# Banded attention's output: one bank-wide copy, two stored halves, and a later sum in memory

## The chip, the cores and the metric

The kernel runs on one core of a Trainium2 chip. The core has five engines that run beside each other and wait for one another by semaphores: TensorE (PE, with its weight loads shown apart as PEld), VectorE (DVE), ScalarE (ACT), GpSimd (POOL) and SyncE (SP). In this kernel SP alone issues the memory transfers (DMAs), strictly in order, and sixteen DMA engines carry them out. PSUM is the small memory that TensorE writes and that DVE and ACT read; SBUF is the working memory of 128 partitions; DRAM is the large memory outside. The metric is device time in microseconds (us).

## The reference

The kernel computes one decoder layer on 2048 tokens of width 1024 behind 16 meta tokens. Cut to what matters:

```python
xn = rms_norm(h, norm_gain[l])
proj = xn @ w_in[l]
sb_q, sb_k, sb_v, sw_q, sw_k, sw_v, sb_z, sw_z, g_sb, g_sw = jnp.split(proj, offsets, axis=-1)
o_sb = stick_breaking_attention(sb_q, sb_k, sb_v, valid)              # 8 heads of 64
o_sw = sliding_window_sink_attention(q, k, sw_v, attn_sinks[l], valid) # 16 query heads, 2 kv heads
y_sb = (o_sb * jax.nn.silu(sb_z)) @ w_branch_sb[l]
y_sw = (o_sw * jax.nn.silu(sw_z)) @ w_branch_swa[l]
merged = jax.nn.sigmoid(g_sb) * y_sb + jax.nn.sigmoid(g_sw) * y_sw
h = h + merged @ w_out[l]
return rms_norm(h, final_norm_gain)[:, BLOCK:]
```

The change concerns `o_sw`, the banded attention's output before it is gated by `sw_z`: within a block of 128 queries, probabilities over the block and the one before it, times the values, for 16 heads of 64.

## The kernel before, in words

All matrix products run on TensorE in three passes: every operand is split into a rounded high part and a low part (the remainder), and high times high, high times low and low times high are added up in one PSUM bank of 128 partitions by 512 columns. The tokens are four groups `g` of 512, taken in two halves: half 0 is groups 2 and 3, half 1 is groups 0 and 1 (the sequence is stored backwards, so half 0 is the end with the meta tokens).

The stages, in the order of the program: a start (projections for the first keys, values and queries); the banded attention of half 0 (`window`, woven among projections); the stick-breaking attention of half 0 (`stick`, woven among the gate projections); the remaining gates of half 0; the banded attention of half 1; the stick-breaking attention of half 1; the last gates of half 1; and `finish`, which takes half 0 (groups 2 and 3) and then half 1 through the branch projections, the output projection and the last norm.

What sets the order of the work: TensorE's order is fixed by the program text (`weave` mixes a main and a side stream by estimated costs), in the whole kernel. The orders of DVE, ACT, POOL and SP are chosen when the kernel is built, by a planner that follows a simulated timeline, except at the start, where they are partly written out. On the chip each engine then takes its instructions strictly in that order, so an instruction that waits holds all behind it. Tiles of one name rotate through a fixed number of buffers (`bufs`); a new tile waits until the buffer's last reader is done.

The banded attention works in units (head set `s` of four heads, group `g`, block `i`), 64 in all, 32 in each half. A unit goes through `scores` (products in bank `z`, copies to `sc` on ACT and DVE, maximum and exponentials, L691 to L716), three units later through `turn` (transposes in bank `t`, the split into `ph` and `pl`, L736 to L747) and then `values` (L749 to L773): six matmuls (L761) fill the single PSUM bank `o`. The value operand holds high parts in 64 columns and low parts in the other 64, so that bank rows 0 to 63 are the product with the high values and rows 64 to 127 that with the low values; their sum is the output. ACT copies rows 64 to 127 to SBUF (L763), and two DVE additions (L767), one for each parity of the head, add rows 0 to 63 and write the tile `os` (128 by 2 by 512, one buffer). After the fourth unit of a group two DMAs of 256 KB store `os` to the DRAM tiles `ow`, of which there are 32 (head pair `k` of 8, group `g` of 4). The next unit's matmuls need the bank `o` back, that is, both additions done.

`gated` (L194) later loads an `ow` tile and its gate `zw`, multiplies them and splits the product into the projection's operands. It does this for half 0's sixteen tiles during the last gates of half 1, and for half 1's sixteen in `finish`, after each half-0 group's output. For the stick-breaking output `od`, which is stored as a high and a low tile (L201 adds them), it does the same with one load and one DVE addition more.

`finish` runs, for half 0: 16 branch projections of 24 matmuls (d of 8, g of 2), multiplied by the gate `gt` loaded from `gw` (L259), with all of `gated(od)` at d = 3; then 16 projections of 12 matmuls, multiplied and merged (L267, L268, L270, L271), each d followed by a load and a split of an output weight tile (`out_weights`, L242 and L243); then the output products (L288 to L290). Staging tiles `a` have six buffers (AB), `gt` three; PSUM results rotate over six banks.

In `stick`, `row` makes a row of scores (L862, L866) and scans it on DVE (L876), five rows ahead of `turn` in half 1, and `tmp` tiles (nine buffers) serve as staging.

Of the kernel before, what the change touches and what calls it, by code (L numbers as in the profile page):

```python
# [7 lines left out]
F32 = mybir.dt.float32  # L8
# [3 lines left out]
ALU = mybir.AluOpType  # L12
# [4 lines left out]
P = 128  # L17
# [4 lines left out]
GT = 512  # L22
# [11 lines left out]
AB = 6  # L34
# [13 lines left out]
def tile_kernel(ctx, tc, x, xt, meta, metat, gain, w_in, w_sb, w_sw, w_out, sinks, fgain,  # L48
# [6 lines left out]
    V, A, G, T = nc.vector, nc.scalar, nc.gpsimd, nc.tensor  # L55

    def DMA(dst, src):
        nc.sync.dma_start(*(t.bitcast(F32) if t.dtype == F32R else t for t in (dst, src)))
# [28 lines left out]
    def dram(name, shape, dt=F32):  # L87
        return dp.tile(shape, dt, tag=name, name=name)
# [6 lines left out]
    gs = [[dram(f"gs{p}_{g}", [P, GT]) for g in range(4)] for p in range(8)]  # L95
    gw = [[dram(f"gw{p}_{g}", [P, GT]) for g in range(4)] for p in range(8)]
    od = [[dram(f"od{p}_{g}", [2, P, GT]) for g in range(4)] for p in range(4)]
    ow = [[dram(f"ow{p}_{g}", [P, GT]) for g in range(4)] for p in range(8)]
    ksv = dram("ksv", [P, 4, P], F32R)
    msd = [dram(f"msd{p}", [NM, P]) for p in range(2)]  # L100
    vsv = dram("vsv", [P, 2 * P], F32R)
# [88 lines left out]
    def rings():  # L190
        lp = cst.enter_context(tc.tile_pool(name="cl", bufs=1, side="left"))
        return lambda dt=F32R: lp.tile([P, GT], dt, tag="L", name="ringl", bufs=32)

    def gated(src, zz, k, g, ring, stg):  # L194

        a, b = stg(), stg()
        if src is od:
            c = stg()
            DMA(a, src[k][g][0])
            DMA(c, src[k][g][1])  # L200
            V.tensor_tensor(a, a, c, op=ALU.add)  # L201
        else:
            DMA(a, src[k][g])
        DMA(b, zz[k][g])
        V.tensor_tensor(a, a, b, op=ALU.mult)
        h, l = ring(), ring()
        A.copy(h, a)
        V.tensor_tensor(l, a, f32(h), op=ALU.subtract)
        return h, l

    def finish(ringl, osw, first):
# [6 lines left out]
        def ringr(dt=F32R):  # L218
            return cp.tile([P, GT], dt, tag="R", name="ringr", bufs=32)
# [7 lines left out]
        def project(acc, ws, ox):  # L227
            nk = len(ox)
            for k in range(nk):
# [2 lines left out]
                T.matmul(acc, lhsT=wh[:, k, :], rhs=l, start=False, stop=False)  # L232
                T.matmul(acc, lhsT=wl[:, k, :], rhs=h, start=False, stop=k == nk - 1)  # L233

        for half, groups in enumerate(halves):
            part, merged, wo = {}, {}, {}

# [10 lines left out]
            for d, g in order:  # L248
                if d == 3 and g == groups[0]:
                    osb = {(k, g): gated(od, zs, k, g, ringr, lambda: small("a", AB)) for g in groups for k in range(4)}  # L250
                if d not in ws_of:
                    ws_of[d] = first if half == d == 0 else weights(d * P, w_sw)
                ws = ws_of[d]
                acc = bank()
                project(acc, ws, [osw[k, g] for k in range(8)])
                gt = small("gt", 3)
                DMA(gt, gw[d][g])
                part[d, g] = ringr(F32)
                V.tensor_tensor(part[d, g], acc, gt, op=ALU.mult)  # L259
            for d in range(8):  # L260
                ws = weights(d * P, w_sb)
                for g in groups:
                    acc = bank()
                    project(acc, ws, [osb[k, g] for k in range(4)])
                    gt = small("gt", 3)
                    DMA(gt, gs[d][g])
                    V.tensor_tensor(gt, acc, gt, op=ALU.mult)  # L267
                    V.tensor_tensor(gt, gt, part[d, g], op=ALU.add)  # L268
                    mh, ml = merged[d, g] = ringl(), ringl()
                    A.copy(mh, gt)  # L270
                    V.tensor_tensor(ml, gt, f32(mh), op=ALU.subtract)  # L271
                out_weights(d, 0)
            for g in groups:
                for t0 in range(0, 4, 2):
# [33 lines left out]
                    for t in (t0, t0 + 1):  # L308
                        row = g * GT + t * P
                        if end and t == 3:  # L310
# [7 lines left out]
                            a, b = scaled_by[0], scaled_by[1]  # L318
# [23 lines left out]
    def tmp(dt=F32, rows=P):  # L342
        return tp.tile([rows, GT], dt, tag="tmp", name="tmp", bufs=9)
# [259 lines left out]
    def window(half, groups, sp):  # L603
# [145 lines left out]
        def values(s, g, i, st):  # L749
            kv = s // 2  # L750
            blk = 4 * (g - groups[0]) + i
            if i == 0:
                os_[0] = sp.tile([P, 2, GT], F32, tag="os", name="os", bufs=1)
            o = ps("o")
            ph, pl, pm = st["p"]
            oc = o.rearrange("p (a q) -> p a q", a=4)
            for n in range(2):
                c = slice(HB * n, HB * n + HB)
                v = vv[:, blk + n, kv, :]
                for j, (lv, rp) in enumerate(((v, ph), (v, pl), (dv[kv, blk][:, n, :], pm))):  # L760
                    T.matmul(oc[:, :, c], lhsT=lv, rhs=rp[:, :, c], start=j == 0, stop=j == 2)  # L761
            t = tmp(rows=64)
            A.copy(t, o[64:128])  # L763
            ov = o[0:64].rearrange("p (b a q) -> p b a q", b=2, a=2)
            tv = t.rearrange("p (b a q) -> p b a q", b=2, a=2)
            for a in range(2):
                V.tensor_tensor(os_[0][64 * a:64 * a + 64, :, i * P:(i + 1) * P],  # L767
                                ov[:, :, a, :], tv[:, :, a, :], op=ALU.add)
            if i == 3:
                for pr in range(2):  # L770
                    DMA(ow[2 * s + pr][g], os_[0][:, pr, :])

        os_ = [None]  # L773
        ending = []
# [21 lines left out]
        return sw_k, sw_v, sw_q, attend, ending  # L796


    def stick(groups, bp):
        kt, vc = {}, {}  # L800
        rows_of = {}
        lt = LT[groups[0] == 0]
# [30 lines left out]
        def load_q(h, g):  # L833
            p, a = divmod(h, 2)
            r = slice(64 * a, 64 * a + 64)
            q1 = bp.tile([P, GT], F32R, tag="q1", name="q1", bufs=2)
            q2 = bp.tile([P, GT], F32R, tag="q2", name="q2", bufs=2)
            for t in range(2):
                DMA(q1[64 * t:64 * t + 64], qd[p][g][t][r])
                DMA(q2[64 * t:64 * t + 64], qd[p][g][1 - t][r])  # L840
            return q1, q2

        state = {}

        def row(h, g, n, j):

            if n == j == 0:
                load_kv(h, g)
                state[h, g] = {"q": load_q(h, g), "last": {}}
            st = state[h, g]  # L850
            last = st["last"]
            b0 = 4 * (g + n) + j
            nb = min(4, NB - b0)
            end = b0 + nb == NB
            w = nb * P + (NM if end and nb < 4 else 0)
            k0 = (b0 - 4 * groups[0]) * P
            own = end and nb == 4
            z = ps("z")
            zm = ps("zm") if own else None
            for t, qt in enumerate(st["q"]):  # L860
                lq = qt[:, j * P:(j + 1) * P]
                T.matmul(z[:, :w], lhsT=lq, rhs=kt[h][:, k0:k0 + w], start=t == 0, stop=t == 1)  # L862
                if own:
                    T.matmul(zm[:, :NM], lhsT=lq, rhs=kt[h][:, k0 + w:k0 + w + NM], start=t == 0, stop=t == 1)
            r = bp.tile([P, RW], F32, tag="row", name="row", bufs=12)
            A.activation(r[:, :w], z[:, :w], AF.Sigmoid, scale=-1.0)  # L866
            if own:
                A.activation(r[:, w:w + NM], zm[:, :NM], AF.Sigmoid, scale=-1.0)
                w += NM
            if n == 0 and mask is None:  # L870
                G.affine_select(out=r[:, :P], in_=r[:, :P], pattern=[[1, P]], compare_op=ALU.is_ge,  # L871
                                fill=1.0, base=-1, channel_multiplier=-1)
            if n == 0 and mask is not None:
                V.tensor_tensor_scan(r[:, :w], r[:, :w], mask[:, :w], 1.0, op0=ALU.mult, op1=ALU.max)  # L874
            else:
                V.tensor_tensor_scan(r[:, :w], r[:, :w], r[:, :w], last[j] if n else 1.0, op0=ALU.mult, op1=ALU.min)  # L876
            last[j] = r[:, w - 1:w]
            rows_of[h, g, n, j] = r
# [44 lines left out]
        n = len(steps)  # L923
        turned = []
        for s in range(n + lt + 3):
# [3 lines left out]
            t = s - lt  # L929
# [164 lines left out]
    halves = ([2, 3], [0, 1])  # L1094
# [160 lines left out]
    for half, groups in enumerate(halves):  # L1255
        gts = [lambda spec=spec: gate(*spec) for spec in specs[half]]
        with tc.tile_pool(name=f"swa{half}", bufs=1, side="left") as sp:
# [13 lines left out]
            q = [[lambda p=p: sw_q(p) for p in (2 * s, 2 * s + 1)] for s in range(4)]  # L1271
# [22 lines left out]
            else:  # L1294
                for mk, gs_ in ((sw_k, groups), (sw_v, groups), *((f, groups[:1]) for f in q[0])):
                    w, use, _ = mk()
# [6 lines left out]
            side = attend()  # L1303
# [8 lines left out]
            early = first_sums(*groups, short)  # L1312
        with tc.tile_pool(name=f"sb{half}", bufs=1, side="left") as bp:
            hsplit[0], vsplit[0] = True, False
            side = stick(groups, bp)
            drain(tiles_by_tile(gts[few:few + 1], groups))
            rest = 28 - FAST - PLAIN if half == 0 else 23
            cost_sb = 8 * sum(4 * (4 - g) for g in groups) * 1.31 + 16 * 0.75 + LT[half] * 0.86
            ratio = cost_sb / ((rest - few - 1) * 10.4)
            weave(tiles_by_tile(gts[few + 1:rest], groups), side, ratio)  # L1320
            if half == 0:
                hsplit[0] = vsplit[0] = True
                plain = [mk() for mk in gts[rest:rest + 2]]
            drain(side)
        if half == 0:
            with tc.tile_pool(name="fast", bufs=1, side="left") as bp:
                pairs = list(zip(specs[0][-FAST::2], specs[0][-FAST + 1::2]))
                sums_x = combined(*groups, bp, short, *early)
                with tc.manual_schedule(engines={mybir.EngineType.Activation}):
                    for n in range(PLAIN):  # L1330
                        w, use, _ = plain[n]
# [86 lines left out]
```

## Time and profile before

| what | value |
|---|---|
| median of three runs | 2139.83 us (2138.06 to 2143.08) |
| the profiled execution | 2139.65 us |
| its span (first to last instruction) | 2138.0 us |
| PE busy | 2111.4 us (99%) |
| DVE busy | 1460.2 us (68%) |
| ACT busy | 1078.6 us (50%) |
| POOL busy | 307.7 us (14%) |
| DMA traffic | 390.93 MB, mean 183 GB/s |
| granted TensorE clock | full in all stages |

The profile page gives busy times, a row for each group of instructions and the chain of work that ended last. The trace behind it answers for any stretch of the span (in us from its start), any line or any tile. A wait is named by what ended it. Matmuls overlap: one of 512 columns reads 0.39 us, while the next may start 0.23 us after it. Half 0's banded attention lies at about 100 to 373 us, half 1's at 840 to 1104, half 1's stick-breaking at 1104 to 1615, half 0's part of `finish` at 1683 to 1880.

### The profile page before, as it was taken

What the parts mean: (1) busy time and instruction counts of PE and PEld (TensorE: products, weight loads), DVE (VectorE), ACT (ScalarE), POOL (GpSimd) and SP (SyncE); (2) the same over time, 40 slices, a digit from 0 to 9 for tenths busy, and PEclk for the clock granted to TensorE, in tenths of its full rate; (3) what the DMA queues carried; (4) which work ended last, traced back from release to release, by engine and by line L of the source; (5) the groups of instructions that cost most, each with busy time, mean ns of one, the idle gap of its engine ahead of it and who ended that gap; (6) DMA issues with size and microseconds to landing.
All of it is one profiled execution on the core that took longest, in us unless ns stands there. A gap on an engine that the chain in (4) does not pass through costs nothing.

```text
span 2138.0 us, 30784 instructions
## 1 busy us (share of the span) xinstructions
PE 2111.4 (99%) x10658; PEld 1751.4 (82%) x10658; DVE 1460.2 (68%) x2335; ACT 1078.6 (50%) x2461; POOL 307.7 (14%) x494
## 2 busy tenths in 40 slices
PE   8999999999999999999999999999999999999998
PEld 6788888888888888888888888888888888787886
DVE  7788876878887554777738888877774447454553
ACT  6576775555546335777735555555553213221121
POOL 2234453111000001343310000000000121000000
PEclk9999999999999999999999999999999999999999
DMA  9755554756448574435354434333324986568422
GB/s 337 276 191 191 177 193 165 242 181 200 153 156 326 213 254 154 148 138 175 134 178 152 123 124 131 113 116 108 113 90 172 359 288 209 172 221 308 149 94 89
DMA packets 170043, 390.93 MB, mean 183 GB/s; under 512 B 24448, under 2 KB 28288, under 8 KB 169888
## 3 DMA queue, kind: packets, MB, share of 16 engines
q1 hardware_dynamic: 169888, 388.97, 54.0%
q8 instruction: 84, 1.38, 0.3%
q14 instruction: 71, 0.58, 0.1%
HBM read 241.55 MB, written 145.18 MB: 181 GB/s over the span
## 4 chain that ended last, share of the span: by engine, by line
PE 84%; DVE 5%; ACT 4%; issue 3%; DMA 2%; POOL 1%; SPq 0%; POOLq 0%; ACTq 0%; DVEq 0%
PE ps_g L412 11%; PE ps_g L413 11%; PE ps_g L414 11%; PE ps_o L913 6%; PE ps_z L862 6%; PE ps_t L887 6%; PE ps_z L705 2%; PE ps_o L761 2%; PE ps_g L233 1%; PE ps_g L232 1%; PE ps_g L231 1%; PE ps_z L233 1%; PE ps_z L231 1%; PE ps_z L232 1%; PE ps_t L233 1%
## 5 line engine op out<-in xcount | busy, mean ns | idle before, releaser
L412 PE MATMUL ps_g<-xh,wh 128*128 128x512 f32 x1296 | 532.9, 411 | 8.7 <-ACT xh L1107 6.8
L414 PE MATMUL ps_g<-xh,wl 128*128 128x512 f32 x1296 | 509.7, 393 | 0.6 <-DVE wl L111 0.6
L413 PE MATMUL ps_g<-xl,wh 128*128 128x512 f32 x1296 | 509.2, 393 | 0.0
L876 DVE TENSOR_TENSOR_SCAN row<-row 128x512 f32<-128x512 f32 (+4 forms) x256 | 293.6, 1147 | 93.3 <-ACT row L866 40.3
L414 PEld LDWEIGHTS ps_g<-xh,wl 128*128 128x128 f32 x1296 | 243.8, 188 | 55.6 <-DVE wl L111 1.1
L412 PEld LDWEIGHTS ps_g<-xh,wh 128*128 128x128 f32 x1296 | 244.9, 189 | 48.5 <-ACT xh L1107 6.8
L866 ACT ACTIVATE row<-ps_z 128x512 f32<-128x512 f32 (+1 forms) x320 | 172.4, 539 | 211.8 <-PE ps_z L862 191.4
L413 PEld LDWEIGHTS ps_g<-xl,wh 128*128 128x128 f32 x1296 | 245.1, 189 | 38.2 <-DVE xl L1108 1.3
L114 ACT ACTIVATE wth<-ps_t 128x512 fp32r<-128x512 f32 (+1 forms) x320 | 170.6, 533 | 75.8 <-PE ps_t L887 74.0
L115 DVE SCALAR_TENSOR_TENSOR wtl<-ps_t,wth 128x512 fp32r<-128x512 f32 (+1 forms) x320 | 189.1, 591 | 25.5 <-ACT wth L114 25.1
L862 PE MATMUL ps_z<-kt,q 128*128 128x512 f32 (+3 forms) x640 | 185.5, 370 | 0.0
L887 PE MATMUL ps_t<-ident,row 128*128 128x128 f32 x1088 | 171.6, 273 | 0.1
L887 PEld LDWEIGHTS ps_t<-ident,row 128*128 128x128 f32 x1088 | 134.6, 140 | 33.7 <-DVE wtl L115 0.8
L862 PEld LDWEIGHTS ps_z<-kt,q 128*128 128x128 f32 x640 | 117.9, 188 | 23.8
L913 PE MATMUL ps_o<-wth,vc 128*128 128x512 f32 (+1 forms) x320 | 130.3, 407 | 0.2
L913 PE MATMUL ps_o<-wtl,vc 128*128 128x512 f32 (+1 forms) x320 | 116.7, 365 | 0.0
L713 ACT ACTIVATE sc<-sc,nm 128x129 f32<-128x129 f32 x256 | 100.0, 393 | 31.4 <-DVE nm L711 30.3
L111 POOL TENSOR_TENSOR wl<-raw,wh 128x1024 fp32r<-128x1024 f32 (+1 forms) x28 | 60.3, 2155 | 325.4 <-ACT wh L108 287.6
L871 POOL TENSOR_SCALAR_AFFINE_SELECT row<-row 128x128 f32<-128x128 f32 x64 | 20.3, 318 | 469.4 <-ACT row L866 442.2
L108 ACT CAST wh<-raw 128x1024 fp32r<-128x1024 f32 (+1 forms) x44 | 42.7, 971 | 87.9 <-PE ps_g L232 35.5
L874 DVE TENSOR_TENSOR_SCAN row<-row,mask 128x512 f32<-128x512 f32 (+2 forms) x64 | 67.9, 1066 | 19.6 <-ACT row L866 11.5
L567 ACT ACTIVATE tmp<-ps_g 128x512 f32<-128x512 f32 x84 | 50.2, 598 | 61.6 <-PE ps_g L414 55.3
(435 smaller groups left out, 4118.0 us busy)
## 6 DMA issues: line engine op xcount, KB each, us to landing
wh<-h_in_w_in SPq DMA_DIRECT2D x66, 512.0 KB, 3.6
wl<-l_in_w_in SPq DMA_DIRECT2D x66, 512.0 KB, 4.8
raw<-in_w_in SPq DMA_DIRECT2D x50, 512.0 KB, 5.6
h_in_w_in<-wh SPq DMA_DIRECT2D x50, 512.0 KB, 2.9
l_in_w_in<-wl SPq DMA_DIRECT2D x50, 512.0 KB, 4.0
q<-qd SPq DMA_DIRECT2D x128, 128.0 KB, 3.1
vc<-vd SPq DMA_DIRECT2D x48, 256.0 KB, 2.9
kd<-tmp SPq DMA_DIRECT2D x32, 256.0 KB, 3.8
```

What stands on the lines that cost most here:

```text
L114: A.activation(h, acc, AF.Copy, scale=scale)
L115: V.scalar_tensor_tensor(l, acc, scale, f32(h), op0=ALU.mult, op1=ALU.subtract)
L412: T.matmul(acc, lhsT=wh[:, k, :], rhs=xh[g][:, k, :], start=k == 0, stop=False)
L413: T.matmul(acc, lhsT=wh[:, k, :], rhs=xl[g][:, k, :], start=False, stop=False)
L414: T.matmul(acc, lhsT=wl[:, k, :], rhs=xh[g][:, k, :], start=False, stop=k == KT - 1)
L713: A.activation(sc[:, hh, :], sc[:, hh, :], AF.Exp, bias=nm[:, hh:hh + 1], accum_out=den[:, hh:hh + 1])
L862: T.matmul(z[:, :w], lhsT=lq, rhs=kt[h][:, k0:k0 + w], start=t == 0, stop=t == 1)
L866: A.activation(r[:, :w], z[:, :w], AF.Sigmoid, scale=-1.0)
L874: V.tensor_tensor_scan(r[:, :w], r[:, :w], mask[:, :w], 1.0, op0=ALU.mult, op1=ALU.max)
L876: V.tensor_tensor_scan(r[:, :w], r[:, :w], r[:, :w], last[j] if n else 1.0, op0=ALU.mult, op1=ALU.min)
L887: T.transpose(tr[:, j * P:(j + 1) * P], rows_of[h, g, n - (j > i), j][:, k0:k0 + P], ident)
L913: T.matmul(o[:, :n], lhsT=v, rhs=r, start=first and r is wh, stop=last)
```

## The change

In `values`, ACT copies the whole bank (128 by 512) at once into `os`, which now has the shape 128 by 4 heads by 256 columns (two units, the same number of bytes, still one buffer). The 64-row copy and both DVE additions are gone. After every second unit four DMAs of 128 KB each (64 partitions, runs of 1 KB) store the high rows to `ow[k][g][0]` and the low rows to `ow[k][g][1]`; the `ow` tiles are twice as large.

A new function `closed` loads both parts of one `ow` tile (256 KB each), adds them on DVE and stores the sum over the high part (256 KB). It is called 32 times. Half 0's sixteen tiles are closed in half 1's `stick`, in `row`, at the starts of head and group pairs: none at the first two, two at the third, one at each later one and one more at the eighth. Half 1's sixteen are closed in half 0's part of `finish`: eight in the branch loop for d of 4 to 7 (one for each d and group), eight in the merge loop, one for each d. `gated` then loads part 0 as it did before.

```diff
-    ow = [[dram(f"ow{p}_{g}", [P, GT]) for g in range(4)] for p in range(8)]
+    ow = [[dram(f"ow{p}_{g}", [2, P, GT]) for g in range(4)] for p in range(8)]
...
+    def closed(k, g, stg):
+
+        a, b = stg(), stg()
+        DMA(a, ow[k][g][0])
+        DMA(b, ow[k][g][1])
+        V.tensor_tensor(a, a, b, op=ALU.add)
+        DMA(ow[k][g][0], a)
+
     def gated(src, zz, k, g, ring, stg):
 
         a, b = stg(), stg()
+        DMA(a, src[k][g][0])
         if src is od:
             c = stg()
-            DMA(a, src[k][g][0])
             DMA(c, src[k][g][1])
             V.tensor_tensor(a, a, c, op=ALU.add)
-        else:
-            DMA(a, src[k][g])
...
+        open_ = [(k, g) for g in halves[1] for k in range(8)]
...
                 DMA(gt, gw[d][g])
+                if half == 0 and d > 3:
+                    closed(*open_.pop(0), lambda: small("a", AB))
...
                     V.tensor_tensor(gt, gt, part[d, g], op=ALU.add)
+                    if half == 0 and g == groups[0]:
+                        closed(*open_.pop(0), lambda: small("a", AB))
...
-            if i == 0:
-                os_[0] = sp.tile([P, 2, GT], F32, tag="os", name="os", bufs=1)
+            if i % 2 == 0:
+                os_[0] = sp.tile([P, 4, 2 * P], F32, tag="os", name="os", bufs=1)
...
-            t = tmp(rows=64)
-            A.copy(t, o[64:128])
-            ov = o[0:64].rearrange("p (b a q) -> p b a q", b=2, a=2)
-            tv = t.rearrange("p (b a q) -> p b a q", b=2, a=2)
-            for a in range(2):
-                V.tensor_tensor(os_[0][64 * a:64 * a + 64, :, i * P:(i + 1) * P],
-                                ov[:, :, a, :], tv[:, :, a, :], op=ALU.add)
-            if i == 3:
+            A.copy(os_[0][:, :, i % 2 * P:(i % 2 + 1) * P], oc)
+            if i % 2:
                 for pr in range(2):
-                    DMA(ow[2 * s + pr][g], os_[0][:, pr, :])
+                    for n in range(2):
+                        DMA(ow[2 * s + pr][g][n][:, (i - 1) * P:(i + 1) * P].rearrange("(a d) t -> d a t", a=2),
+                            os_[0][64 * n:64 * n + 64, 2 * pr:2 * pr + 2, :])
...
-    def stick(groups, bp):
+    def stick(groups, bp, open_=()):
+        open_ = list(open_)
...
                 state[h, g] = {"q": load_q(h, g), "last": {}}
+                for t in open_[:(0, 0, 2, 1)[min(len(state) - 1, 3)] + (len(state) == 8)]:
+                    closed(*t, tmp)
+                    open_.remove(t)
...
-            side = stick(groups, bp)
+            side = stick(groups, bp, half * [(k, g) for g in halves[0] for k in range(8)])
```

## The prediction

> **What bounds the kernel now.** I read the page first (busy times, then the chain that ended last), then busy times by stage, then what TensorE (PE) waited for in the two banded stages, then the chain around single waits. From the page, the busy line and the chain's shares:
>
> ```profile
> PE 2111.4 (99%) x10658; PEld 1751.4 (82%) x10658; DVE 1460.2 (68%) x2335; ACT 1078.6 (50%) x2461; POOL 307.7 (14%) x494
> ...
> PE 84%; DVE 5%; ACT 4%; issue 3%; DMA 2%; POOL 1%; SPq 0%; POOLq 0%; ACTq 0%; DVEq 0%
> ```
>
> TensorE is the bound: 99% busy, 84% of the chain. Its work and order do not change, so a gain can only come out of its waits. Where these lie, the busy times by stage show (us, then busy time and count of PE, PEld, DVE, ACT and POOL, the granted clock, DMA share, GB/s): the banded attention of half 0 from its first output, that of half 1, half 1's stick-breaking, and in the finish the branch loop for d of 4 to 7 and the merge loop.
>
> ```profile
> 130.00:373.00 243.00, 238.96 (x1355) 204.34 (x1354) 190.11 (x375) 170.72 (x498) 108.58 (x185) 1.00 0.52 181
> 889.00:1104.00 215.00, 212.80 (x1172) 183.31 (x1171) 155.78 (x314) 152.81 (x434) 76.52 (x151) 1.00 0.43 147
> 1135.00:1615.00 480.00, 479.94 (x2607) 400.96 (x2606) 385.27 (x466) 264.02 (x515) 17.67 (x60) 1.00 0.37 113
> 1727.00:1772.00 45.00, 45.00 (x194) 36.22 (x193) 16.24 (x20) 5.78 (x9) 7.40 (x4) 1.00 0.66 231
> 1772.00:1817.00 45.00, 45.00 (x194) 36.09 (x193) 37.73 (x53) 16.01 (x28) 8.78 (x6) 1.00 0.72 234
> ```
>
> In the banded stages PE idles 4.04 and 2.20 us, 6.2 together; in the three others it does not idle by more than 0.06. What ended its idle times there, half 0 first, then half 1 (us in total, times, longest):
>
> ```profile
> PE ps_zm L525 <- DVE tmp L115: 1.8, 2, 1.1
> PE ps_o L761 <- DVE os L767: 0.8, 2, 0.6
> PE ps_t L551 <- DVE tmp L518: 0.7, 1, 0.7
> ```
>
> ```profile
> PE ps_o L761 <- DVE os L767: 1.6, 1, 1.6
> PE ps_o L761 <- POOL pm L745: 0.4, 2, 0.2
> ```
>
> The three waits on L767 are PE waiting for the bank `o`, which the two additions free. The chain around one of these shows an addition directly in front (start, us, what):
>
> ```profile
> 186.08 0.43 DVE os L767
> 186.51 0.14 issue
> 186.64 0.36 PE ps_o L761
> ```
>
> Busy rows hide a little of a stall: a matmul reads 0.39 us where the next can start 0.23 later, as two in a row in the finish do, so each wait is 0.16 longer than its idle time.
>
> ```profile
> 1811.68 0.39 PE L233 MATMUL ps_g<-ringr,wl 128*128 128x512 f32 x1
> 1811.91 0.39 PE L231 MATMUL ps_g<-ringr,wh 128*128 128x512 f32 x1
> ```
>
> **The change part by part.** The groups of the removed work, of the nearest copy of a whole bank, and of two additions like the new one (mean ns behind the comma):
>
> ```profile
> L767 DVE TENSOR_TENSOR os<-ps_o,tmp 64x256 f32<-64x256 f32 x128 | 52.8, 413 | 6.8 <-ACT tmp L763 5.8
> L763 ACT COPY tmp<-ps_o 64x512 f32<-64x512 f32 x64 | 37.4, 584 | 17.2 <-PE ps_o L761 15.9
> L917 ACT COPY tmp<-ps_o 128x512 f32<-128x512 f32 x32 | 18.8, 587 | 19.4 <-PE ps_o L913 19.1
> L205 DVE TENSOR_TENSOR a<-a 128x512 f32<-128x512 f32 x32 | 22.0, 689 | 9.2 <-DMA a<-zs 6.9 <-DMA a<-zw 2.0
> L201 DVE TENSOR_TENSOR a<-a 128x512 f32<-128x512 f32 x16 | 14.6, 914 | 12.4 <-DMA a<-od 12.4
> ```
>
> *Removed:* 128 additions by 413 ns, 52.8 us of DVE, all in the banded stages (about 345.9 us of DVE busy there). The bank comes back after the ACT copy alone, some 0.83 us earlier. The least that this is worth is the three waits on L767: 0.8 + 1.6 + 3 × 0.16 = 2.9 us. The most is all idle time of the two stages with 0.16 for each of the eight waits listed: 6.2 + 1.3 = 7.5 us. Other waits there end with DVE as well (the 1.8 on L115, 0.7 on L518), a smaller part with POOL; I take the middle, 5.2 us.
>
> *The wider copy:* 64 copies go from 584 to 587 ns, 0.2 us of ACT, beside PE's projections.
>
> *The stores:* 128 DMAs of 128 KB from 64 partitions instead of 32 of 256 KB. The nearest rows are `od`'s stores of the same size: their issue on SP (ns min/median/max), their landing (last figure, us), and for comparison the landing of the old stores (us min/median/max); then the shortest time between two copies that will have a store between them:
>
> ```profile
> L58 SPq DMA_DIRECT2D od<-tmp x64: 445/512/1115, 406.1 to 1628.2; - x64
> ```
>
> ```profile
> od<-tmp SPq DMA_DIRECT2D x64, 128.0 KB, 2.5
> ```
>
> ```profile
> DMA to landing us min/median/max: 2.0/2.2/3.6
> ```
>
> ```profile
> 313.96 0.59 ACT L763 COPY tmp<-ps_o 64x512 f32<-64x512 f32 x1
> ...
> 318.60 0.59 ACT L763 COPY tmp<-ps_o 64x512 f32<-64x512 f32 x1 [0.33 <-PE ps_o L761]
> ```
>
> `os` has one buffer, so the third unit's copy waits on ACT until the four stores of the pair before have landed: 0.59 for the copy, three issues of 0.51, 2.5 to land, 4.6 us from copy to copy. The shortest gap is 4.64 us; the mean is 243/32 = 7.6 us. So this costs 0, if SP takes the stores up at once. If they land in 3.6 us the need is 5.7, and 31 times the 1.1 us missing at the shortest gap would be 34 us of ACT: the far end, since few gaps are that short. What is queued behind the waiting copy on ACT is the next unit's `ph` and `sc` work, for which PE's transposes and matmuls wait. On SP 96 issues more by 0.51 us are 49 us, spread over 458 us. SP waited 3.4 us for each group before, so it stood ready:
>
> ```profile
> SPq L58 <- DVE os L767: 54.2, 16, 8.4
> ```
>
> *Half 0's sums in stick-breaking:* 16 additions by 0.69 us, 11.0 us on DVE, with 48 DMAs. DVE goes from 385 to 396 of 480 us. The tightest place is the start of a head and group pair, where the transposes follow the scan of the fourth row; one such place:
>
> ```profile
> 1340.39 1.23 DVE L876 TENSOR_TENSOR_SCAN row<-row 128x512 f32<-128x512 f32 x1 [0.96 <-POOL row L871]
> ```
>
> ```profile
> 1344.38 0.60 PE L887 MATMUL ps_t<-ident,row 128*128 128x128 f32 x4
> ```
>
> The scan ends at 1341.62, PE takes its row at about 1344.7: 3 us in hand, against one addition of 0.69. Cost 0; if nothing hid them, 11.0.
>
> *Half 1's sums in the finish:* eight additions in the branch loop, 5.5 us, where DVE idles 45 - 16.24 = 28.8 us: 0. Eight more in the merge loop, 5.5 us, where DVE idles only 7.3 us. And there its lateness is passed on, as the chain behind the loop shows:
>
> ```profile
> 1819.91 0.70 DVE ringl L271
> ...
> 1821.95 5.45 DMA a<-in_w_out
> ```
>
> ```profile
> 1830.02 0.50 PE L289 MATMUL ps_z<-ringr,ringl 128*128 128x512 f32 x1 [0.22 <-DVE ringr L243]
> ```
>
> SP issues the second half of the output weights only behind L271, and PE already waits for them at 1830. So DVE's lag at 1819.91 is paid one for one. Idle time ahead takes seven additions; the last has almost none behind it, so I charge one, 0.7 us (ends: 0 and 5.5). In this loop the sums move 8 × 0.786 MB, 140 GB/s more on 234; the heaviest stretch of the finish carried 385, so this fits, with nothing to spare:
>
> ```profile
> 1690.00:1700.00 10.00, 10.00 (x45) 8.04 (x44) 3.95 (x6) 0.00 (x0) 0.00 (x0) 1.00 1.04 385
> ```
>
> *Sum:* -5.2 for the banded stages, 0 for the copies, 0 for the stores, 0 in stick-breaking, +0.7 in the finish: -4.5 us, on the profiled execution's own 2139.65 (which stands 0.18 below the median): 2135.1 us. What is late next in the banded stages is POOL's `pm` (L745) and ACT's exponentials.
>
> A row that speaks against the change is L201: the same addition, 0.69 us alone, has a mean of 914 ns, and one of it reads
>
> ```profile
> 1716.73 2.89 DVE L201 TENSOR_TENSOR a<-a 128x512 f32<-128x512 f32 x1
> ```
>
> [...]
>
> **The rivals.**
>
> *All of these waits go* (chance 0.14): the earlier bank also lets ACT and POOL start earlier, as the additions stood ahead of so many waits, and the finish hides its sums: -7.5, 2132.1. Against it: the waits on POOL and ACT that are left.
>
> *The freed time does not reach PE* (0.14): only the three bank waits go, since the chain around the others passes to ACT (153 to 171 us busy per stage) and POOL: -2.9 + 0.7, 2137.4, within 0.2% (4.3 us, about what a measurement of this kernel can tell from no change).
>
> *The merge loop falls behind* (0.15): its additions meet POOL's weight splits. At 2.89 us each, eight are 23.1 us against 7.3 idle: a lag of 15.8, paid in full at 1830: -5.2 + 15.8 = +10.6, 2150. It decides for slower when the lag passes 9.5 us, that is from 2.1 us an addition. For it: L201's rows; against: POOL is busy in 8.78 of 45 us.
>
> *The stores hold ACT* (0.11): SP reaches them late, being held by another wait (its longest for `os` alone was 8.4). At 4 us late the need is 8.6 from copy to copy, 1.0 over the mean of 7.6: 31 us of ACT; a third of that on PE, 10 us, with the bank waits back: 2139.65 + 10 = about 2150. It decides from about 3 us late on.
>
> **How the numbers follow.** The forecast's own case (a gain of 3 to 7 us, 2132.7 to 2136.7) has 0.46; three quarters of it lie beyond 0.2%. Faster: 0.34 + 0.14 = 0.48. Within 0.2%: 0.12 + 0.14 = 0.26. Slower: 0.15 + 0.11 = 0.26. The range runs from below the case of all waits, 2130, to 2147, which takes in the milder part of both slower cases.
>
> **What would show it.** In the new profile L767 is gone, and 64 copies of 128x512 near 587 ns stand in its place; DVE's busy time in the banded stages falls by about 25 us each, PE's idle time there from 6.2 to 1 or 2, without a wait on `os` at L761. ACT waits for the `os` stores nowhere. In stick-breaking PE stays without idle time. In the finish the new additions read 0.7 to 0.9 us, L271's last stands within 1 us of where it stood relative to PE, and PE's wait near 1830 grows by less than 1 us. Wrong would be: ACT waiting for stores of `os`; PE waiting at L289 for L243 by several us; a DVE addition blocked on its loads ahead of scans; or new waits because the planner orders ACT, DVE and SP otherwise around the shorter DVE queue, which no row of before can price.

## The result, and the profile after

The changed kernel takes 2147.06 us (median of nine runs, 2144.11 to 2150.31) against 2139.83 for the kernel before on the same chip (nine runs, 2138.06 to 2143.82): a ratio of 1.0031, 95% interval 1.0022 to 1.0041. It became slower by 0.3%; 2135.1 was predicted, in a range from 2130 to 2147. The profiled execution took 2146.06 us, 6.41 more than that of before. The same statements stand up to 11 lines further down in the changed kernel (the bank's matmuls L761 at L772, the output products L288 to L290 at L299 to L301, the merges L267 to L271 at L276 to L282); L773 is the new copy, L199 the addition in `closed`.

First the busy times by stage of the changed kernel, for the five stretches that the prediction showed and two short ones behind them (columns: stretch, its length, busy time and count of PE, PEld, DVE, ACT and POOL, granted clock, DMA share, GB/s):

```profile
130.00:373.00 243.00, 240.41 (x1370) 206.64 (x1369) 171.93 (x317) 168.06 (x500) 110.41 (x186) 1.00 0.63 201
889.00:1104.00 215.00, 214.03 (x1178) 184.76 (x1177) 131.66 (x251) 147.97 (x432) 71.77 (x149) 1.00 0.54 171
1135.00:1615.00 480.00, 479.02 (x2603) 400.13 (x2602) 390.44 (x480) 263.59 (x512) 17.77 (x60) 1.00 0.44 138
1727.00:1772.00 45.00, 45.00 (x194) 36.22 (x193) 21.27 (x28) 4.67 (x7) 6.57 (x5) 1.00 0.90 326
1772.00:1817.00 45.00, 45.00 (x194) 36.08 (x193) 35.38 (x52) 14.58 (x24) 8.17 (x5) 1.00 1.00 357
1817.00:1825.00 8.00, 1.91 (x6) 0.70 (x5) 5.25 (x9) 2.10 (x4) 0.00 (x0) 0.87 0.85 319
1825.00:1832.00 7.00, 6.67 (x19) 4.81 (x20) 4.25 (x7) 2.15 (x5) 0.00 (x0) 0.66 0.68 209
```

In the two banded stages PE now idles 2.59 and 0.97 us, 3.56 instead of 6.2, and DVE is busy 18 and 24 us less. In stick-breaking PE idles 0.98 us instead of 0.06. The merge loop (1772 to 1817) moves 357 GB/s where it moved 234, and its DMA share is 1.00: the sixteen engines are busy all the time. Behind it PE is busy for 1.91 of 8 us.

What ended PE's idle times, in the order of the program: the two banded stages (shown there: only the waits of the `o` bank's matmuls, L772), stick-breaking, finish (us in total, times, longest):

```profile
PE ps_o L772 <- POOL pm L756: 0.8, 1, 0.8
...
PE ps_o L772 <- DVE pl L115: 0.7, 1, 0.7
PE ps_o L772 <- POOL pm L756: 0.2, 1, 0.2
...
PE ps_t L898 <- DVE wtl L115: 1.0, 1, 1.0
...
PE ps_t L299 <- ACT ringl L281: 6.3, 1, 6.3
```

The waits for the bank copy are gone, and one new wait of 6.3 us stands at the first output product that needs the last merged operand. PE executes the same 10658 matmuls in the same order in both kernels, so the start of one and the same matmul can be compared. In the two banded stages PE gains 3.25 and 1.67 us, 4.9 together; about 1.0 is lost again between the two, in a part that the change does not touch. At the end of half 1's banded attention a matmul starts 3.88 us earlier than before (1085.31 against 1089.19), after a stick-breaking wait 2.86 earlier, at the last product ahead of the new wait 2.38 earlier, and ten matmuls on 6.72 later. So 9.1 us are lost in one place.

The chain of waits through that place (start, us, what):

```profile
1808.11 6.09 DMA wl<-l_in_w_sw
...
1814.27 6.57 DMA a<-ow
...
1820.93 0.69 DVE a L199
1821.62 0.54 DVE gt L276
...
1823.53 0.63 ACT ringl L281
```

and PE beside it, in order of time (start, us, engine, line, operation; in brackets the idle time before it and what ended it):

```profile
1825.24 0.80 PE L299 MATMUL ps_t<-ringr,ringl 128*128 128x512 f32 x1 [6.33 <-ACT ringl L281]
1826.12 0.79 PE L300 MATMUL ps_t<-ringr,ringl 128*128 128x512 f32 x1
1826.72 0.80 PE L301 MATMUL ps_t<-ringr,ringl 128*128 128x512 f32 x1
1827.32 0.63 PE L299 MATMUL ps_g<-ringr,ringl 128*128 128x512 f32 x1
1827.74 0.63 PE L300 MATMUL ps_g<-ringr,ringl 128*128 128x512 f32 x1
```

The chain runs through memory: a load of a projection weight takes 6.09 us, the load of the last sum 6.57, and L199, the new addition, holds DVE until it has landed (2.58 us of idle time before it):

```profile
1820.93 0.69 DVE L199 TENSOR_TENSOR a<-a 128x512 f32<-128x512 f32 x1 [2.58 <-DMA a<-ow]
```

Only then follow the last merges, on which the output products wait. After the gap PE is also slow for some 4.6 us: matmuls start 0.88, then 0.60, then 0.43 us apart instead of 0.23; the granted clock is 0.66 on average over 1825 to 1832. That makes 6.6 us for the wait and 2.5 for the slow matmuls.

How crowded memory is, the gate's loads show, 256 KB each, from 1772 to 1830: first the kernel before, then the changed one (tile, queue, count, KB, median us from issue to landing):

```profile
gt<-gs SPq DMA_DIRECT2D x14, 256.0 KB, 2.8
```

```profile
gt<-gs SPq DMA_DIRECT2D x13, 256.0 KB, 5.7
```

### The profile page after: what moved, and what is told of

Read it like the earlier page. It is cut to its first block, busy times and chain, and to the rows that moved or that the text cites. A ratio compares the mean times of both kernels' runs of the same rounds, so it can differ in the third digit from the quotient of the medians.

```text
span 2144.3 us, 30930 instructions
## 1 busy us (share of the span) xinstructions
PE 2112.5 (99%) x10658; PEld 1752.1 (82%) x10658; DVE 1431.3 (67%) x2239; ACT 1071.6 (50%) x2461; POOL 304.4 (14%) x494
## 4 chain that ended last, share of the span: by engine, by line
PE 87%; DVE 4%; ACT 3%; issue 2%; DMA 2%; POOL 1%; SPq 0%; ACTq 0%; POOLq 0%; DVEq 0%
PE ps_g L423 12%; PE ps_g L424 12%; PE ps_g L425 12%; PE ps_o L924 6%; PE ps_z L873 6%; PE ps_t L898 5%; PE ps_z L716 2%; PE ps_o L772 2%; PE ps_g L239 1%; PE ps_g L238 1%; PE ps_z L239 1%; PE ps_g L237 1%; PE ps_z L238 1%; PE ps_z L237 1%; PE ps_t L239 1%
## 5 line engine op out<-in xcount | busy, mean ns | idle before, releaser
L111 POOL TENSOR_TENSOR wl<-raw,wh 128x1024 fp32r<-128x1024 f32 (+1 forms) x28 | 61.6, 2201 | 326.0 <-ACT wh L108 209.7
```

## The experiments

Ratios are to the kernel before on the same chip; 0.1% is 2.1 us. Three explanations were at hand. The loss comes from the merge loop's sums because memory is full there; or because the additions take DVE's time or meet POOL (the prediction's rival); or because an addition standing in DVE's order waits for its own loads. And the banded gain might not have come at all.

In the kernels that alter only the finish, DVE, ACT, POOL and SP have the order of the kernel that they start from until the finish. Inside the finish the planner orders DVE, ACT and SP anew for each kernel, so a sum does not always run where the program text has it; where that matters, the times are given.

**Without the merge loop's sums.**

```diff
                     V.tensor_tensor(gt, gt, part[d, g], op=ALU.add)
-                    if half == 0 and g == groups[0]:
-                        closed(*open_.pop(0), lambda: small("a", AB))
```

> The changed kernel with the eight sums of the merge loop left out: the low parts of the banded output's group 1 are never added, so the output lacks them. Theory A (the merge loop's sums make TensorE wait at the first output product): its 6.3 us wait for the merged tile of d = 7 goes, and with it the slower matmuls behind it at a granted clock of 0.66, about 9 us together: 2138 us, 0.1% under the kernel before. Theory B (the loss lies elsewhere, in the stores, the stick-breaking sums or the new order, and would show at another wait): 2145 to 2147 us.

Measured: 2136.00 us, ratio 0.9984 (0.9975 to 0.9992). The merge loop moves 270 GB/s at a share of 0.81, and PE's waits behind it are 0.5 us. About 10 us (0.47%) hang on these eight sums.

**The additions alone, on data that lies in SBUF.**

```diff
-                        closed(*open_.pop(0), lambda: small("a", AB))
+                        e = small("a", AB)
+                        V.tensor_tensor(e, fg[:, :GT], fg[:, GT:], op=ALU.add)
```

> As the run without the merge loop's sums, but in each one's place a DVE addition of the same size (128x512) on tiles that are already in SBUF: DVE's time without the transfers; the low parts of the banded output's group 1 are left out again. If the wait comes from an addition standing in DVE's queue for its loads, this is as fast as without sums: 2138 us, no wait of TensorE over 1 us at the first output product. If DVE's time is the cause (the prediction's rival: eight additions against the loop's idle time, slowed by POOL), the wait stays at 4 us or more and the time is 2143 to 2147 us.

Measured: 2137.02 us, 0.9987 (0.9977 to 0.9996). The stretch 1772 to 1817 of this kernel:

```profile
1772.00:1817.00 45.00, 45.00 (x195) 36.08 (x194) 39.71 (x58) 16.29 (x29) 8.12 (x5) 1.00 0.81 278
```

DVE is busy 39.71 of 45 us, more than in the changed kernel, POOL is as busy as there (8.12 and 8.17), and PE waits for no more than 0.7 us behind the loop. But without loads to wait for, the planner starts five of the eight additions ahead of 1772, from 1761.7 on, and the last at 1784.0, while the changed kernel's run from 1774.9 to 1820.9. So this kernel shows that the additions fit in, and not what they would cost at the loop's end; that the loss does not need them, the next kernel shows.

**The transfers alone, without the addition.**

```diff
-                        closed(*open_.pop(0), lambda: small("a", AB))
+                        e, f = small("a", AB), small("a", AB)
+                        k1, g1 = open_.pop(0)
+                        DMA(e, ow[k1][g1][0])
+                        DMA(f, ow[k1][g1][1])
+                        DMA(ow[k1][g1][0], e)
```

> As the run without the merge loop's sums, but with the three transfers of each sum (two loads, one store of 256 KB) and no addition; the low parts of the banded output's group 1 are left out again. If the addition's wait in DVE's queue is the cause, most of the loss goes: about 2139 us. If the fuller DMA engines alone are the cause (the loads of gates and weights come late), the loss stays: 2144 to 2147 us, with TensorE waiting at the first output product for 4 us or more.

Measured: 2149.05 us (four runs), 1.0043 (1.0029 to 1.0056). Stretches, PE's wait, and the load on the chain:

```profile
1772.00:1817.00 45.00, 45.00 (x194) 36.08 (x193) 32.02 (x43) 13.47 (x23) 7.18 (x6) 1.00 1.00 356
...
1825.00:1832.00 7.00, 1.87 (x4) 1.06 (x5) 6.12 (x10) 2.46 (x4) 0.00 (x0) 0.50 0.22 66
```

```profile
PE ps_t L303 <- ACT ringl L285: 9.0, 2, 5.6
```

```profile
1818.62 6.45 DMA a<-in_w_out
```

The loss is all there without an addition, so neither the additions' time on DVE nor their meeting POOL is needed for it. What now stands in DVE's order and waits is the split of an output weight (L250), whose load took 6.45 us. So it is the traffic: the explanation by the addition waiting for its own loads falls as the cause, and stays as the way in which a late load reaches PE. Here another instruction that DVE reaches in order and that needs a load does the same. The transfers also hold two of the six staging buffers `a` for each sum, and this kernel does not separate the two; the gate's loads, which go to buffers of their own, are late as well (5.7 us above, and in the next kernel).

**Half of them, and all of them, later.** In one kernel four of the merge loop's sums move to the output products of group 2, in the other all eight; nothing is left out.

```diff
-                    if half == 0 and g == groups[0]:
+                    if half == 0 and g == groups[0] and d % 2 == 0:
                         closed(*open_.pop(0), lambda: small("a", AB))
...
+                            if half == 0 and g == groups[0] and ch:
+                                closed(*open_.pop(0), lambda: small("a", AB))
```

> Four of the merge loop's eight sums stay there (every second d), four move to the output products of half 0's first group; nothing is left out. The merge loop's transfers without sums made 270 GB/s, with eight 357, at a DMA share of 1.00. If the loss begins where the DMA engines are full, four sums (about 314 to 340 GB/s) cost nothing or little: 2137 to 2139 us. If every sum costs its share, half of the loss is left: about 2141 to 2142 us.

```diff
-                    if half == 0 and g == groups[0]:
-                        closed(*open_.pop(0), lambda: small("a", AB))
...
+                            if half == 0 and g == groups[0]:
+                                closed(*open_.pop(0), lambda: small("a", AB))
```

> The changed kernel with the eight sums of the merge loop called one by one in the output products of half 0's first group instead, where the DMA engines were busy for about half of the time; nothing is left out. Theory A: as fast as without those sums, 2138 us, under both kernels but within 0.2% of the one before. If sums cost what they cost wherever they stand in the finish: 2144 to 2147 us.

Measured: with half of them later 2143.72 us, 1.0016 (1.0007 to 1.0025); with all of them later 2137.23 us, 0.9987 (0.9978 to 0.9995). The kernel with half of them, its stretches, its wait, and its chain ahead of the wait:

```profile
1772.00:1817.00 45.00, 45.00 (x195) 36.07 (x194) 36.42 (x52) 15.30 (x26) 6.46 (x5) 1.00 0.95 327
1817.00:1825.00 8.00, 3.73 (x12) 2.63 (x11) 6.07 (x10) 1.87 (x4) 0.00 (x0) 0.78 0.47 138
1825.00:1832.00 7.00, 7.00 (x26) 5.50 (x25) 2.04 (x4) 3.24 (x7) 0.00 (x0) 0.77 0.90 297
```

```profile
PE ps_t L299 <- ACT ringl L281: 4.3, 1, 4.3
```

```profile
1807.95 6.03 DMA gt<-gs
1815.31 4.46 DMA gt<-gs
```

At a share of 0.95 some 6 us of the loss remain (0.29% over all of them later), more than the half that four sums would have by an equal share, and here the gate's own loads are late. With all of them later the merge loop runs at 0.80 and 269 GB/s, and the output products, at 277 GB/s, carry the sums without a wait:

```profile
1772.00:1817.00 45.00, 45.00 (x195) 36.08 (x194) 37.46 (x54) 15.86 (x28) 6.46 (x5) 1.00 0.80 269
...
1832.00:1880.00 48.00, 48.00 (x208) 38.60 (x207) 27.22 (x58) 10.34 (x29) 0.00 (x0) 1.00 0.81 277
```

That version is 0.13% faster than the kernel before and 0.44% faster than the changed one.

**Without any sum.**

```diff
-                if half == 0 and d > 3:
-                    closed(*open_.pop(0), lambda: small("a", AB))
...
-                    if half == 0 and g == groups[0]:
-                        closed(*open_.pop(0), lambda: small("a", AB))
...
-            side = stick(groups, bp, half * [(k, g) for g in halves[0] for k in range(8)])
+            side = stick(groups, bp)
```

> The changed banded attention alone: the bank-wide copy and the two stores, with all 32 later sums left out, so the low parts of the banded output are missing. The profile of the changed kernel puts its gain in the banded stages at 3 to 4 us and a loss of about 1 us in the stick-breaking of half 1: if that is right, 2135 to 2136 us, and TensorE has no wait for a split behind a sum near 1325 us. If the prediction's middle of 5.2 us holds, 2134.7 or less; if the stores cost something that the sums' absence does not show, 2138 or more.

Measured: 2134.53 us, 0.9974 (0.9964 to 0.9984). The copies and stores of the banded part are worth 5.6 us (3.4 to 7.7), and all sums together cost 0.57%, 12 us.

**The sums in the kernel before.** As many loads, additions and stores, the stores to memory of their own, in the merge loop of the kernel before.

```diff
+    scr = [dram(f"scr{p}", [P, GT]) for p in range(8)]
...
+                    if half == 0 and g == groups[0]:
+                        e, f = small("a", AB), small("a", AB)
+                        DMA(e, ow[d][halves[1][1]])
+                        DMA(f, ow[d][halves[1][0]])
+                        V.tensor_tensor(e, e, f, op=ALU.add)
+                        DMA(scr[d], e)
```

> The kernel before, with the eight loads of two tiles, additions and stores put into its merge loop as the changed kernel has them, on a piece of memory of their own, so that the output stays the reference's; nothing else is changed. If the loss belongs to these sums alone, whatever the banded attention does, about 9 us over the kernel before: 2147 to 2151 us, with TensorE's wait at the first output product. If it needs something else of the change (the branch loop's sums ahead of it, a later start), under 2143 us.

Measured: 2143.68 us, 1.0013 (1.0004 to 1.0022). Only some 3 us, a third of the loss. The branch loop and the merge loop of this kernel suggest why there is less:

```profile
1727.00:1772.00 45.00, 45.00 (x195) 36.19 (x194) 19.67 (x24) 4.67 (x7) 8.28 (x5) 1.00 0.83 291
1772.00:1817.00 45.00, 45.00 (x195) 36.07 (x194) 37.42 (x53) 16.05 (x27) 6.57 (x5) 1.00 0.89 292
```

A good part of the new transfers ran ahead into the branch loop (291 instead of 231 GB/s; five of the eight additions start ahead of 1772), which in the changed kernel is full of its own eight sums. So this does not test eight sums inside the merge loop.

**Without the branch loop's sums**, with those of the merge loop kept:

```diff
                 if half == 0 and d > 3:
-                    closed(*open_.pop(0), lambda: small("a", AB))
+                    open_.pop(0)
```

> The changed kernel with the merge loop's eight sums kept and the branch loop's eight left out (the low parts of the banded output's group 0 are missing). Without the merge loop's sums the branch loop's cost next to nothing; this asks whether the merge loop's cost their 10 us alone. If they do: 2145 to 2147 us. If the two add up, because the branch loop's sums take the staging buffers in which the output weights were fetched ahead and so move 1.5 MB of loads into the merge loop: about 3 us over the kernel that has no sums in the finish, some 2139 us, with the first loads of the output weights before 1750 us as in the kernel before, and below 330 GB/s in the merge loop.

Measured: 2139.47 us, 0.9998 (0.9988 to 1.0007): taking away the sums at which PE did not wait at all brings back 0.33%, 7 us. But again five of the eight additions that are left start ahead of 1772, and the merge loop now stands at 0.88 and 295 GB/s. Over the kernel without sums, these eight and stick-breaking cost 0.24%, and the branch loop's eight and stick-breaking 0.10% in the first experiment; in the changed kernel all sums cost 0.57%. So eight sums nearly fit into the two loops, and sixteen do not. What eight would cost inside the merge loop alone, no kernel here shows.

One trace of each kernel says the same. By the start of one and the same matmul, PE loses between 1720 and 1840, against the kernel before: 0.6 us in the first experiment (share of the merge loop 0.81), 0.9 with all of the loop's sums later (0.80), 1.6 here (0.88), 4.4 with the sums in the kernel before (0.89), 6.6 with half of them later (0.95), 9.2 in the changed kernel and 12.7 with the transfers alone (both 1.00).

The loads of output weights between 1725 and 1830 show what is pushed back, in the changed kernel, in this one, and in the first experiment, which keeps the branch loop's sums alone (count, issue ns min/median/max, first and last issue):

```profile
L58 SPq DMA_DIRECT2D a<-in_w_out x14: 333/431/542, 1770.1 to 1829.4; - x14
```

```profile
L58 SPq DMA_DIRECT2D a<-in_w_out x16: 327/410/888, 1739.9 to 1826.7; - x16
```

```profile
L58 SPq DMA_DIRECT2D a<-in_w_out x16: 327/424/498, 1762.8 to 1823.2; - x16
```

With the branch loop's own sums, which take two of the six staging buffers `a` each, the first output weight is loaded 23 us later, and with the merge loop's sums behind them 30 us. Ahead of 1772 four output weights are loaded here, five in the first experiment, and one in the changed kernel: there, what ran ahead of the merge loop now runs in it. Whether the buffers or the branch loop's transfer rate (326 GB/s, share 0.90) sets this was not separated.

**Stick-breaking: spread, and loads ahead.** Both start from the version with all merge sums later, which has a wait of 0.6 us left in stick-breaking. The first moves the second sum of the eighth pair to the second pair; the second issues the loads one head and group pair ahead of the addition.

```diff
-                for t in open_[:(0, 0, 2, 1)[min(len(state) - 1, 3)] + (len(state) == 8)]:
+                for t in open_[:(0, 1, 2, 1)[min(len(state) - 1, 3)]]:
```

> The kernel with the merge loop's sums moved behind it, and in the stick-breaking of half 1 no place with two sums but the third: one at the second head and group pair in place of the second one at the eighth; nothing is left out. If the 1 us lost at the eighth pair comes from the second sum there, standing in DVE's queue for its loads, the time falls by that, to about 2136.2 us; if the tight start of the stage takes it back, 2137 us or more.

```diff
+                for c, t in loaded:
+                    closed(*c, None, t)
+                del loaded[:]
-                for t in open_[:(0, 0, 2, 1)[min(len(state) - 1, 3)] + (len(state) == 8)]:
-                    closed(*t, tmp)
+                for t in open_[:(0, 2, 2, 1)[min(len(state) - 1, 3)]]:
+                    loaded.append((t, fetched(*t, tmp)))
```

> The kernel with the merge loop's sums moved behind it; in the stick-breaking of half 1 each sum's loads are issued one head and group pair ahead of its addition and store (two at the second and third pair, one at each from the fourth to the fifteenth); nothing is left out. If the stage's loss comes from additions that stand in DVE's queue for their loads, the waits of TensorE in it go (1.0 to 1.8 us): about 2136 us. If the additions' own time or the traffic is the cause, no change: 2137 us and a wait of 0.6 us or more at the transposes.

Measured: spread 2138.72 us, 0.9991 (0.9982 to 1.0000), no better than without; loads ahead 2142.26 us, 1.0011 (1.0002 to 1.0020), worse by about 5 us than the version that both start from. Both were expected near 2136. The waits in stick-breaking, of the spread kernel and of the one with loads ahead:

```profile
PE ps_t L898 <- DVE wtl L115: 1.8, 2, 1.7
```

```profile
PE ps_t L907 <- DVE wtl L115: 5.3, 1, 5.3
```

and DVE in the second at that place, then the chain there:

```profile
1138.91 0.69 DVE L204 TENSOR_TENSOR tmp<-tmp 128x512 f32<-128x512 f32 x1 [4.06 <-DMA tmp<-ow]
...
1141.24 1.31 DVE L896 TENSOR_TENSOR_SCAN row<-row 128x528 f32<-128x528 f32 x1
```

```profile
1120.87 7.99 DMA wl<-l_in_w_in
...
1128.87 6.68 DMA kt<-kd
...
1135.59 4.60 DMA tmp<-ow
```

The loads were earlier in the program but not on the chip: SP got to them only behind a weight and the keys, while the planner had the additions take their turn on DVE, ahead of a scan. Both kernels put sums near the start of half 1's stick-breaking, where the stage's own loads keep memory busy (1104 to 1135 in the kernel before: DMA share 0.87, 276 GB/s), so neither tests whether a sum with its data in place would be free. At the eighth pair itself, with one sum in place of two, the spread kernel waits for 0.2 us instead of 0.6; the 1.7 us are those of the new place.

## Why the prediction was wrong

By its own steps:

- *The banded stages, -5.2 (ends -2.9 and -7.5): right.* PE's gain there is 4.9 us in the traces (3.25 and 1.67), and 5.6 (3.4 to 7.7) in the times of the kernel without sums. PE's idle time fell less than named, from 6.24 to 3.56 and not to 1 or 2. The waits for the bank copy are gone, and what is late next is POOL's `pm`, as named, and DVE; the exponentials of ACT, also named, are not among the waits.
- *The copies and the stores, 0: right.* The 64 copies read 586 ns (median); the stores land in 2.4 us, and ACT waited for them 2.2 us in two places, PE never:

```profile
L773 ACT COPY os<-ps_o x64: 558/586/607, 133.6 to 1099.1; 128x512 f32<-128x512 f32 x64
...
  DMA ow<-os: 2.2, 2
...
DMA to landing us min/median/max: 2.4/2.4/4.3
```

  The rival by which the stores hold ACT falls with that.
- *Stick-breaking, 0: too low by 1 to 2.* The 3 us in hand were compared with one addition of 0.69. At the eighth pair two sums come together, and DVE stood in front of the first until its data came, then needed 0.69 and 0.68 for the two, and PE waited 1.0 us (in the traces of the kernels that keep these sums as they are, the stage costs 1.0 to 1.9):

```profile
1325.03 0.69 DVE L199 TENSOR_TENSOR tmp<-tmp 128x512 f32<-128x512 f32 x1 [1.86 <-DMA tmp<-ow]
...
1327.18 0.68 DVE L199 TENSOR_TENSOR tmp<-tmp 128x512 f32<-128x512 f32 x1
```

- *The branch loop, 0, and the merge loop, +0.7 (ends 0 and 5.5): the steps that failed.* They were priced by DVE's idle time, and the memory's rate was looked at for one loop by itself: "this fits, with nothing to spare", because 234 and 140 GB/s, 374 together, are less than the 385 of the heaviest stretch. The merge loop then carried 357, and the 8 us behind it 319. The 385 was a stretch of 10 us whose share was 1.04: it shows what the DMA engines can carry, not in what time a load then lands. The merge loop needs its gates and output weights soon after they are issued, with three and six buffers for them. With the share at 1.00 the time to land doubled (2.8 to 5.7 us), a DVE instruction stood waiting for a late load, and the wait passed to PE through the merges. The two loops' sixteen sums cost about 10 us, eight of them much less in the traces (0.6 the branch loop's, 1.6 the merge loop's, five of which ran ahead); the branch loop's price was taken as 0 because nothing in it waits, while its sums took the place of what was to run ahead.
- *"DVE's lag at 1819.91 is paid one for one": right that it is paid, by another path and at a higher price.* Expected was PE waiting at L289 for the second half of the output weights, which SP issues behind L271. PE waited earlier, at the first output product, for the merged operand itself (L299 for L281); then came 2.5 us at a reduced clock, for which the sum had no term.
- *The rival "the merge loop falls behind" (2150)* had the place and came near the time by luck, by a wrong cause: the transfers without additions cost everything, and eight additions alone, most of them run early, 0.03% over none. The 2.89 us at which it priced an addition were taken, in the kernel before, beside a weight split of POOL (L111) that had begun 0.27 us ahead, and another addition (L201, 1706.14) took 2.07 us beside the split from 1705.26 to 1707.66:

```profile
1716.46 2.61 POOL L111 TENSOR_TENSOR wl<-raw,wh 128x1024 fp32r<-128x1024 f32 x1 [3.20 <-ACT wh L108]
```

  Of the changed kernel's sixteen additions in the finish two began 0.10 us after such a split (at 1769.36 and 1774.95) and took 1.73 and 1.74 us; the other fourteen took 0.68 or 0.69, and the median is 692 ns, against the rival's 2890 for each. So this is not what decided here:

```profile
L199 DVE TENSOR_TENSOR a<-a x16: 680/692/1740, 1740.3 to 1820.9; 128x512 f32<-128x512 f32 x16
```

The sum with measured terms, in times: -5.6 for the banded stages and +12.2 for the sums gives +6.6, the 0.31% of the result; as both terms are taken from the same kernel without sums, this must come out. The traces divide the 12.2: 9.2 in the two loops of the finish (the kernel without sums gains 0.5 there), 1.2 in stick-breaking; the rest lies within the intervals.

## What to carry to other kernels

Work that is moved to where an engine is idle still has to be paid in that stage's transfers and buffers (here about 10 us for the two loops' sixteen sums): add up its bytes with those of the neighbouring loops, and treat a DMA share near 0.9 with suspicion when the stage's loads are needed within a few microseconds: in this loop 0.88 and 0.89 cost 1.6 and 4.4 us, 0.95 cost 6.6. Loads that would have run ahead are part of the price, and here it fell due in the next stage, not where the sums stood. An instruction that reads a fresh load should stand behind those that the bound engine needs, since every engine takes its instructions in order (here the last merges stood behind L199, which waited 2.58 us for its load); that was not tested by itself.

## What the runs showed of the hardware

Not expected was how dear a single gap on TensorE is. After idle times of 6.3, 5.6 (the longer of two) and 4.3 us, the clock granted in the stretch 1825 to 1832 was 0.66, 0.50 and 0.77 on average (the changed kernel, the transfers alone, half of the sums later). In the changed kernel one step stands behind the average, to half: PE's last matmul ended at 1818.9, the clock was 1.00 until 1822, 0.97 over 1822 to 1823 and 0.50 from there, so it dropped about 4 us into the gap, and the matmuls' 0.43 us from start to start are nearly twice the 0.23.

```profile
1823.00:1829.70 6.70, 4.38 (x9) 2.97 (x10) 5.48 (x9) 3.00 (x6) 0.00 (x0) 0.50 0.49 157
```

In the kernel with loads ahead, a gap of 5.3 us did the same:

```profile
1142.00:1149.00 7.00, 6.21 (x23) 5.42 (x24) 4.75 (x8) 1.49 (x3) 0.00 (x0) 0.55 0.32 94
1149.00:1156.00 7.00, 7.00 (x39) 5.76 (x38) 5.06 (x6) 3.97 (x7) 0.88 (x3) 1.00 0.69 206
```

In the seven microseconds after that the clock is full again. A gap of 1.7 us (the spread kernel) left it at full:

```profile
1140.00:1143.00 3.00, 3.00 (x17) 2.46 (x16) 1.83 (x3) 1.90 (x4) 0.29 (x1) 1.00 0.85 207
```

So in these kernels a gap of 1.7 us left the clock at full, and gaps of 4.3 us and more were followed by a lower one; what lies between was not measured by itself. In the changed kernel about 2.5 us came on top of the 6.3 us gap, and the full clock came back after some 4.6 us of work (0.62 over 1829 to 1830, 1.00 over 1830 to 1831).
